# An encoder block in fp32 halves on one core: mixer tiles at a new address, norm 2 and the mixer's operands in a new order, some sums on GpSimd

## The chip, the cores and the metric

The kernel runs on one core of a Trainium2 chip. The metric is the device time of one execution in microseconds (us), as the median of several runs. In the profile PE is TensorE's matmul side, PEld its weight loads, DVE is VectorE, ACT is ScalarE, POOL is GpSimd and SP is SyncE, which issues most of the DMAs.

## What is computed

One layer of a hybrid encoder on 1024 tokens (and 16 meta tokens) of width 1024. The change touches the end of the block alone:

```
h  = h + mix @ w_out              # mix: merged attention and recurrent branches
hn = rmsnorm(h, norm2_g)          # "norm 2"
gu = hn @ w_ffn_in                # 1024 -> 2 x 2816
g, u = gu[..., :D_FF], gu[..., D_FF:]
h  = h + (silu(g) * u) @ w_ffn_out
```

## The kernel before

Every matrix product is made of three matmuls: each fp32 operand is split into a rounded high half (`hi`, by ACT) and a remainder (`lo = source - hi`, by DVE, or by GpSimd where the helper `split` is told so), and the product is hi\*hi + hi\*lo + lo\*hi. All three are matmuls of a 128x128 stationary operand (the weights of PE) with a 128x512 moving operand.

The program runs in stages: projections and the recurrent branch (to about 490 us of the span), attention (490 to 820 us), the output projection `w_out` with norm 2 (797 to 918 us), the mixer's first half `ffn_in` (918 to 1340 us), and its second half (1340 to 1550 us). The names in the trace:

- The output projection adds to the residual rows of token tile t (0 to 7, 128 tokens each) in four parts: two column halves n and two contraction halves kh. Its PSUM tiles are `oph`, `S` and `ops`, and DVE adds each to `h`.
- `norm2_rows(t)` norms the eight tiles one by one (`ss`, `nv`, `ns`, `nr`, `ne` are its small columns, `y` its result). PE then transposes `y` into two PSUM tiles `hT`.
- The mixer uses Strassen's scheme in Winograd's form (7 products in place of 8). The lower tokens (tiles 0 to 3) give the operands B11 and B21 directly (`B`). For each upper tile (4 to 7), `norm2_T` makes c1 to c4 and c22 out of the transposed rows and the lower tile's values, which GpSimd first puts together again from their halves (`whole`), and splits them into T1 to T4 and B22 (`T`, `B`).
- For each of 22 blocks f of 128 mixer columns, `prep(f)` loads the weights (`raw`), forms the sums s1 to s4 (`s`) and splits seven weight operands (`wA`, `wS`). `early(f)` makes the two products that need only the lower tokens (A11 with B11, A12 with B21); `ffn_in(f)` makes the other five (S2 with T2 first, then S3, S1, A22, S4). A product is 12 matmuls.
- The second half of the mixer has the products `po`, whose two operands both lie in one page `pw`.

The normed tokens `xn` lie in two chunks: the first has the 16 meta tokens ahead of its 512 (rows of 528 columns), the second 512 alone. The projections `gm`, `gr` and others of the early stages use both in turn, with one set of weights `wblk`.

The big operands lie in 15 *pages* of SBUF (`xn`, `wblk`, `M`, `wo`, `B`, `T`, `pw`). The mixer's weights lie in a pool of 12 tiles `t4` (4 KB per partition), its temporaries in a pool of 10 tiles `t2`. The order of the instructions on each engine is the one in which the program was built: an engine waits with its next instruction until that can run. Before the change the eight tiles are normed one per output tile in the last eight output tiles, `norm2_T` follows one tile behind, and the two products of `early` for the blocks 0 and 1 stand ahead of the last two `norm2_T`.

Of the kernel before, what the change touches and what calls it, by code (L numbers as in the profile page):

```python
# [8 lines left out]
F32 = mybir.dt.float32  # L9
# [4 lines left out]
ALU = mybir.AluOpType  # L14
# [12 lines left out]
DFF = 2816  # L27
# [8 lines left out]
N_PAGES = 15  # L36
N_T4 = 12
N_T2 = 10


@with_exitstack
def tile_hybrid_encoder_block(
# [258 lines left out]
    ys = [norm1_rows(0)]  # L301
# [219 lines left out]
    for b in range(NB):  # L521
# [5 lines left out]
        w = next_block()  # L527
# [139 lines left out]
    def out_half(t, n, kh, ps):  # L667

        c, o = t // 4, 128 * (t % 4)
        for j in range(2):  # L670
            w = wo[2 * kh + j, n]
            for k in range(2):
                lh, ll = (M[hl][kh][c][:, 2 * j + k, o:o + 128] for hl in range(2))
                PE.matmul(out=ps, lhsT=lh, rhs=w[:, k, 0], start=(j == 0 and k == 0), stop=False)
                PE.matmul(out=ps, lhsT=lh, rhs=w[:, k, 1], start=False, stop=False)
                PE.matmul(out=ps, lhsT=ll, rhs=w[:, k, 0], start=False, stop=(j == 1 and k == 1))
            if j == 1:
                hs = hres[t][:, 512 * n:512 * n + 512]
                V.tensor_tensor(out=hs, in0=hs, in1=ps, op=ALU.add)
            yield  # L680
# [43 lines left out]
    for _ in steps:  # L724
        pass
    load_mix(0, 1)
    for k in range(8):
        if k % 2 == 0 and pend:
            u = pend.pop(0)
            emit_pv(*u, gar[u[0]])  # L730
        for _ in out_half(k % 4, k // 4, 1, SB[k // 3][:, k % 3] if k < 6 else fill_bank("oph")):
            pass
    load_mix(1, 1)

# [16 lines left out]
    def t2(name):  # L751
        return p3.tile([128, 512], F32, tag="t2", bufs=N_T2, name=name)

# [11 lines left out]
    def hb(name):  # L765
        if name not in HB:
            HB[name] = [page([128, 4, 512], F32R, f"{name}{hl}") for hl in range(2)]
        return HB[name]
# [3 lines left out]
    def norm2_rows(t):  # L772
        y = t4([128, D], F32, "y2")
        norm_rows(hres[t], 128, g2b, y)
        SP.dma_start(out=h_d[t], in_=hres[t])
        return y

    def norm2_T(t, y):
        o = slice(128 * (t % 4), 128 * (t % 4) + 128)
        ps = []  # L780
        for kh in range(2):
            p = bank("hT")
            for k in range(4):
                kk = 4 * kh + k
                PE.transpose(out=p[:, 128 * k:128 * k + 128], in_=y[:, 128 * kk:128 * kk + 128], identity=ident)
            ps.append(p.rearrange("p (k t) -> p k t", k=4))
        if t < 4:
            for n, nm in enumerate(("B11", "B21")):
                hi, lo = hb(nm)
                split(ps[n], hi[:, :, o], lo[:, :, o])  # L790
            return
        b12, b22 = ps

        def tmp(name):
            return t2(name).rearrange("p (k t) -> p k t", k=4)

        def whole(nm):
            b = tmp("whole")
            hi, lo = hb(nm)
            G.tensor_tensor(out=b, in0=f32(hi)[:, :, o], in1=f32(lo)[:, :, o], op=ALU.add)  # L800
            return b

        b11, b21 = whole("B11"), whole("B21")

        def put(nm, src):
            hi, lo = hb(nm)
            split(src, hi[:, :, o], lo[:, :, o])

        c22 = tmp("c22")
        S.activation(out=c22, in_=b22, func=AF.Copy)  # L810
        c1 = tmp("c1")
        V.tensor_tensor(out=c1, in0=b12, in1=b11, op=ALU.subtract)
        c2 = tmp("c2")
        V.tensor_tensor(out=c2, in0=c22, in1=c1, op=ALU.subtract)
        c3 = tmp("c3")
        V.tensor_tensor(out=c3, in0=c22, in1=b12, op=ALU.subtract)
        c4 = tmp("c4")
        V.tensor_tensor(out=c4, in0=b21, in1=c2, op=ALU.subtract)
        for nm, src in (("T2", c2), ("T3", c3), ("T1", c1), ("T4", c4), ("B22", c22)):
            put(nm, src)  # L820

    def out_tile(t, n, kh):
        for _ in out_half(t, n, kh, bank("ops")):
            pass

    for t in range(4, 8):
        hres[t] = t4([128, D], F32, "h")
        SP.dma_start(out=hres[t], in_=x[128 * t:128 * t + 128])
    for n in range(2):
        for t in range(4, 8):  # L830
            out_tile(t, n, 0)
    ys = []

    def lagged(lag):
        while len(ys) > lag:
            norm2_T(*ys.pop(0))

# [4 lines left out]
    act_d = [dram.tile([7, 128, 512], F32, name=f"act_d{j}") for j in range(NFP)]  # L842
    wot_d = [dram.tile([4, 128, 512], F32, name=f"wot_d{j}") for j in range(NFP)]

    def wsplit(f, nm, src):
        w = t4([128, 2, 512], F32R, "w" + nm)
        split(src, w[:, 0], w[:, 1])
        W[f, nm] = w

    def prep(f):  # L850

        raw = []
        for col in (128 * f, DFF + 128 * f):
            r = raw_tile([128, 8, 128])
            SP.dma_start(out=r, in_=w_ffn_in[:, col:col + 128].rearrange("(k p) c -> p k c", p=128))
            raw.append(r.rearrange("p k c -> p (k c)"))
        a11, a12 = raw[0][:, 0:512], raw[0][:, 512:1024]
        a21, a22 = raw[1][:, 0:512], raw[1][:, 512:1024]
        wsplit(f, "A11", a11)
        yield  # L860
        wsplit(f, "A12", a12)
        yield
        s1 = t2("s1")
        V.tensor_tensor(out=s1, in0=a21, in1=a22, op=ALU.add)
        s2 = t2("s2")
        V.tensor_tensor(out=s2, in0=s1, in1=a11, op=ALU.subtract)
        wsplit(f, "S2", s2)
        yield
        s3 = t2("s3")
        V.tensor_tensor(out=s3, in0=a11, in1=a21, op=ALU.subtract)  # L870
        wsplit(f, "S3", s3)
        yield
        wsplit(f, "S1", s1)
        yield
# [94 lines left out]
    def step_prep(f, n=1):  # L969
        if f >= NF:  # L970
            return
        if f not in preps:
            preps[f] = prep(f)
        for _ in range(n):
            next(preps[f], None)

    for t in range(8):
        if t < 7:
            ys.append((t, norm2_rows(t)))
        out_tile(4 + t // 2, t % 2, 1)  # L980
        lagged(1)
        if t == 3:
            step_prep(0, 2)
            step_prep(1, 2)
    ys.append((7, norm2_rows(7)))
    for f in range(2):
        for _ in early(f):
            pass
    lagged(0)
    step_prep(0, 5)  # L990

    for f in range(NF):
# [47 lines left out]
    for n, (i, j) in enumerate(chunks):  # L1040
        if n + AHEAD < len(chunks):
            c = chunks[n + AHEAD]
            pairs[c] = load_pair(*seq[c[0]][:2], c[1])
        w = pairs.pop((i, j))
# [94 lines left out]
```

## Time and profile before

| | us |
|---|---|
| median of 3 runs | 1557.53 (1557.37 to 1559.59) |
| profiled execution, its own time | 1556.03 |
| profiled execution, span of the trace | 1554.3 |
| PE, DVE, ACT, POOL busy in the span | 1493.4, 1094.5, 748.4, 305.9 |
| PE busy from 897 to 918 us | 2.93 of 21.00 |

The span is from the first to the last instruction; 1.7 us of the execution lie around it. A busy PE is not PE at its peak: matmuls overlap each other, and what tells how fast they go is the distance between the starts of two that follow each other, which the text calls the pitch.

### The profile page before, as it was taken

The numbers are of one execution on the slowest core, as the hardware profiler recorded it, in microseconds if no ns is written. First come the engines' busy times: TensorE is split into PE (matmuls) and PEld (weight loads), VectorE is DVE, ScalarE is ACT, GpSimd is POOL, SyncE is SP. The second block draws the span as 40 slices with busy tenths as digits, with TensorE's granted clock in tenths as the row PEclk, the third lists the DMA queues.
The fourth block names the chain that finished last, engine by engine and source line by source line (L and its number), as shares of the span: only waits on it lengthen the run. The fifth ranks groups of instructions, "written<-read, shape, count | busy, mean of one in ns | idle before, by whom it ended". The sixth has DMA issues, their size and how long they took to land.

```text
span 1554.3 us, 20204 instructions
## 1 busy us (share of the span) xinstructions
PE 1493.4 (96%) x7323; PEld 1240.6 (80%) x7323; DVE 1094.5 (70%) x1726; ACT 748.4 (48%) x1266; POOL 305.9 (20%) x229
## 2 busy tenths in 40 slices
PE   6999999999999899998989959999999999999998
PEld 4888888888888788887878848888888888888887
DVE  6888677777776778776754788777777777557562
ACT  5544476666666666665632352323332233364330
POOL 0000000000001444444430203333332333300000
PEclk9999999999999999999999979999999999999999
DMA  6123311111112899999995115444444444798541
GB/s 238 42 78 99 89 41 62 61 61 59 60 55 72 181 202 198 201 197 246 229 237 193 41 42 183 161 156 156 152 151 153 154 153 151 256 386 275 192 160 66
DMA packets 307076, 228.92 MB, mean 147 GB/s; under 512 B 150968, under 2 KB 249232, under 8 KB 306976
## 3 DMA queue, kind: packets, MB, share of 16 engines
q1 hardware_dynamic: 303008, 219.77, 49.7%
q0 software_dynamic: 3968, 7.86, 1.8%
q8 instruction: 57, 0.93, 0.3%
q14 instruction: 43, 0.35, 0.1%
HBM read 135.57 MB, written 56.36 MB: 123 GB/s over the span
## 4 chain that ended last, share of the span: by engine, by line
PE 47%; DVE 2%; DMA 1%; issue 0%; ACT 0%; DVEq 0%
PE po L1055 4%; PE po L1053 4%; PE po L1054 4%; PE S2T L889 1%; PE S2T L887 1%; PE S2T L888 1%; PE S3T L889 1%; PE A22T L889 1%; PE S1T L889 1%; PE S4B L889 1%; PE S4B L888 1%; PE A22T L888 1%; PE S1T L888 1%; PE S3T L888 1%; PE S3T L887 1%; PE S4B L887 1%
## 5 line engine op out<-in xcount | busy, mean ns | idle before, releaser
L594 DVE SCALAR_TENSOR_TENSOR PP<-p,pr,PP 128x1024 f16<-128x1024 f32 (+1 forms) x128 | 120.1, 991 | 18.7 <-ACT PP L591 18.6
L93 ACT ACTIVATE pw<-pr 128x1024 fp32r<-128x1024 f32 x77 | 80.6, 1062 | 104.7 <-PE po L1055 72.2
L93 ACT ACTIVATE wS<-s 128x512 fp32r<-128x512 f32 x88 | 53.1, 628 | 161.3 <-DVE s L870 62.1
L1053 PE MATMUL po<-pw 128*128 128x512 f32 x308 | 119.8, 389 | 0.0
L1055 PE MATMUL po<-pw 128*128 128x512 f32 x308 | 119.8, 389 | 0.0
L1054 PE MATMUL po<-pw 128*128 128x512 f32 x308 | 119.8, 389 | 0.0
L608 PE MATMUL pv<-PT,vt 128*128 128x256 f16 x800 | 99.3, 284 | 17.5 <-DMA PT<-PP 17.5
L94 DVE TENSOR_TENSOR pw<-pr,pw 128x1024 fp32r<-128x1024 f32 x77 | 91.8, 1226 | 32.8 <-ACT pw L93 31.0
L608 PEld LDWEIGHTS <-vt 128*128 128x128 f16 x800 | 78.7, 102 | 34.2 <-issue 18.4
L585 ACT ACTIVATE p<-S,nm 128x1044 f32<-128x1044 f32 x64 | 72.2, 1128 | 66.7 <-DVE nm L582 63.9
L94 DVE TENSOR_TENSOR wS<-s,wS 128x512 fp32r<-128x512 f32 x88 | 70.7, 824 | 19.4 <-ACT wS L93 18.3
L591 ACT ACTIVATE PP<-p,pr 128x1040 f16<-128x1040 f32 x64 | 73.9, 1155 | 13.4 <-DMA PT<-PP 8.7
L582 DVE TENSOR_REDUCE nm<-S 128x1 f32<-128x1044 f32 x64 | 76.9, 1231 | 2.4 <-PE S L101 2.3
L430 POOL MEMSET xrp<- 128x2 f32 x8 | 0.9, 109 | 350.2 <-DVE xc L437 350.2
L99 PE MATMUL S<-kT,qh 128*128 128x348 f32 (+1 forms) x192 | 63.1, 328 | 5.6 <-ACT p L585 5.5
L1054 PEld LDWEIGHTS po<-pw 128*128 128x128 f32 x308 | 57.8, 188 | 12.1
L1055 PEld LDWEIGHTS po<-pw 128*128 128x128 f32 x308 | 57.8, 188 | 12.0
L1053 PEld LDWEIGHTS po<-pw 128*128 128x128 f32 x308 | 57.8, 188 | 11.9
L94 DVE TENSOR_TENSOR wA<-raw,wA 128x512 fp32r<-128x512 f32 x66 | 58.5, 886 | 7.3 <-ACT wA L93 7.3
L100 PE MATMUL S<-kT,qh 128*128 128x348 f32 (+1 forms) x192 | 62.2, 324 | 0.0
L101 PE MATMUL S<-kT,qh 128*128 128x348 f32 (+1 forms) x192 | 62.0, 323 | 0.0
L100 PE MATMUL xr<-xn,wblk 128*128 128x264 f32 (+1 forms) x192 | 61.4, 320 | 0.0
(304 smaller groups left out, 4443.3 us busy)
## 6 DMA issues: line engine op xcount, KB each, us to landing
raw<-in_w_in_dram SPq DMA_DIRECT2D x44, 512.0 KB, 3.9
raw<-in_w_ffn_in_dram SPq DMA_DIRECT2D x44, 512.0 KB, 4.7
pr<-act_d SPq DMA_DIRECT2D x77, 256.0 KB, 5.2
raw<-in_w_ffn_out_dram SPq DMA_DIRECT2D x22, 512.0 KB, 4.0
wot_d<-bs SPq DMA_DIRECT2D x44, 256.0 KB, 4.5
act_d<-as SPq DMA_DIRECT2D x44, 256.0 KB, 2.0
pr<-wot_d SPq DMA_DIRECT2D x44, 256.0 KB, 5.1
act_d<-act SPq DMA_DIRECT2D x33, 256.0 KB, 3.5
```

Source lines behind the costliest of these rows:

```text
L93: S.activation(out=hi, in_=src, func=AF.Copy)
L94: (eng or V).tensor_tensor(out=lo, in0=src, in1=f32(hi), op=ALU.subtract)
L100: PE.matmul(out=ps, lhsT=lh, rhs=rl, start=False, stop=False)
L582: V.tensor_reduce(out=nm, in_=s[:, :, 0:KC], axis=AX.XY, op=ALU.max, negate=True)
L591: S.activation(out=pair[:, 0:NK], in_=pf, func=AF.Copy, scale=r)
L594: V.scalar_tensor_tensor(out=pair[:, o:o + e - a], in0=pf[:, a:e], scalar=r, in1=pair[:, a:e], op0=ALU.mult, op1=ALU.subtract)
L608: PE.matmul(out=ps, lhsT=vt[:, j, hl, vs], rhs=pt[:, m], start=(n == 0), stop=(n == len(terms) - 1))
L888: PE.matmul(out=ps, lhsT=lh, rhs=bl[:, k], start=False, stop=False)
L889: PE.matmul(out=ps, lhsT=ll, rhs=bh[:, k], start=False, stop=k == 3)
L1053: PE.matmul(out=banks[t], lhsT=lh, rhs=w[:, 0, 1], start=j == 0, stop=False)
L1054: PE.matmul(out=banks[t], lhsT=lh, rhs=w[:, 1, 1], start=False, stop=False)
L1055: PE.matmul(out=banks[t], lhsT=ll, rhs=w[:, 0, 1], start=False, stop=j == NFP - 1)
```

## The change

Four things are done.

1. A tile of 96 bytes that nobody uses is put into a small pool, ahead of the pools that hold `raw`, the keys and values, and the mixer's `t4` and `t2`. By the addresses in the two built programs, the start of these tiles in a partition, as bytes past a multiple of 256, moves so:

| tiles | before | after |
|---|---|---|
| all pages (`xn`, `wblk`, `M`, `wo`, `B`, `T`, `pw`, `qh`) | 192 | 192 |
| `t4`, `t2` (`wA`, `wS`, `act`, `s`, `c`, `whole`), `raw`, `kT` | 96 | 192 |
| `PP` (probabilities, source of the DMA transposes), `PT` (their result) | 128, 64 | 224, 160 |
| `gw`, `xch` (the recurrent gates' weights and input) | 128, 96 | 224, 192 |

2. Four output tiles move from the attention stage's PSUM banks behind the end of that stage. The lower tiles 0 to 3 are normed first, all four of them, before the last 16 output tiles, and their transposes lie between output tiles. The upper tiles follow one per two output tiles.
3. The weights A11 and A12 of the blocks 0, 1 and 2 (`N_EARLY`) are split ahead of the others, their `lo` on GpSimd in place of DVE, and the two early products of all three blocks, six products, stand between the last transposes, ahead of the first product S2 with T2. For these three blocks A11 and A12 are loaded a second time, for the sums.
4. For each upper tile the sum c4 and the `lo` of T4 move from DVE to GpSimd; c1 and c4 are written over `whole`. T2 and T3 are split first, the rest (`T1`, `T4`, `B22`) after other work.

```diff
@@ small pool
+    small.tile([128, 24], F32, bufs=1, name="shift")
@@ end of the attention stage
-    for k in range(8):
+    for k in range(4):
...
-        for _ in out_half(k % 4, k // 4, 1, SB[k // 3][:, k % 3] if k < 6 else fill_bank("oph")):
+        for _ in out_half(k, 0, 1, SB[k // 3][:, k % 3]):
@@ operands of the upper tiles
-        b11, b21 = whole("B11"), whole("B21")
...
+        c1, c4 = whole("B11"), whole("B21")
         c22 = tmp("c22")
         S.activation(out=c22, in_=b22, func=AF.Copy)
-        c1 = tmp("c1")
-        V.tensor_tensor(out=c1, in0=b12, in1=b11, op=ALU.subtract)
+        V.tensor_tensor(out=c1, in0=b12, in1=c1, op=ALU.subtract)
...
-        c4 = tmp("c4")
-        V.tensor_tensor(out=c4, in0=b21, in1=c2, op=ALU.subtract)
-        for nm, src in (("T2", c2), ("T3", c3), ("T1", c1), ("T4", c4), ("B22", c22)):
-            put(nm, src)
+        G.tensor_tensor(out=c4, in0=c4, in1=c2, op=ALU.subtract)
+        put("T2", t, c2)
+        put("T3", t, c3)
+        yield
+        put("T1", t, c1)
+        put("T4", t, c4, G)
+        put("B22", t, c22)
@@ output tiles, norm 2, early products
-    for n in range(2):
-        for t in range(4, 8):
-            out_tile(t, n, 0)
+    ys = {}
+    for t in range(4):
+        out_tile(t, 1, 1)
+        ys[t] = norm2_rows(t)
+    for t in range(4, 8):
+        out_tile(t, 0, 0)
...
+    def prep_early(f):
+        for nm, a in zip(("A11", "A12"), load_win(128 * f)):
+            wsplit(f, nm, a, G)
...
-    for t in range(8):
-        if t < 7:
-            ys.append((t, norm2_rows(t)))
-        out_tile(4 + t // 2, t % 2, 1)
-        lagged(1)
-        if t == 3:
-            step_prep(0, 2)
-            step_prep(1, 2)
-    ys.append((7, norm2_rows(7)))
-    for f in range(2):
-        for _ in early(f):
-            pass
-    lagged(0)
-    step_prep(0, 5)
+    for t in range(4):
+        out_tile(4 + t, 1, 0)
+        norm2_lower(t, ys.pop(t))
+    upper = {}
+    for t in range(4, 8):
+        for n in range(2):
+            out_tile(t, n, 1)
+        ys[t] = norm2_rows(t)
+        if t < 6:
+            prep_early(t - 4)
+        else:
+            upper[t - 2] = norm2_upper(t - 2, ys.pop(t - 2))
+            next(upper[t - 2])
...
+    run(early(0))
+    prep_early(2)
+    run(upper[4])
+    upper[6] = norm2_upper(6, ys.pop(6))
+    next(upper[6])
+    run(upper[5])
+    run(early(1))
+    step_prep(0, 1)
+    run(upper[6])
+    upper[7] = norm2_upper(7, ys.pop(7))
+    next(upper[7])
+    run(early(2))
+    step_prep(0, 1)
+    run(upper[7])
+    step_prep(0, 5)
```

What stands on DVE for the last upper tile, t = 7, before the change, from its first sum c1 (`c<-hT,whole`) on; the S2 weights of block 0 (`s`, then `wS`) come behind it:

```order
L812 TENSOR_TENSOR c_8373<-hT,whole 128x512
L94 TENSOR_TENSOR B_8164<-c_8371,B_8163 128x4x128
L814 TENSOR_TENSOR c_8375<-c_8371,c_8373 128x512
L816 TENSOR_TENSOR c_8377<-c_8371,hT 128x512
L818 TENSOR_TENSOR c_8379<-whole,c_8375 128x512
L94 TENSOR_TENSOR T_8148<-c_8375,T_8147 128x4x128
L94 TENSOR_TENSOR T_8152<-c_8377,T_8151 128x4x128
L94 TENSOR_TENSOR T_8156<-c_8373,T_8155 128x4x128
L94 TENSOR_TENSOR T_8160<-c_8379,T_8159 128x4x128
L864 TENSOR_TENSOR s_8391<-raw 128x512
L866 TENSOR_TENSOR s_8393<-s_8391,raw 128x512
L870 TENSOR_TENSOR s_8398<-raw 128x512
```

On DVE for the same tile now, from its c1 (written over `whole`) on:

```order
L818 TENSOR_TENSOR whole<-hT,whole 128x512
L820 TENSOR_TENSOR c_8386<-c_8383,whole 128x512
L97 TENSOR_TENSOR wS_8360<-s_8358,wS_8360 128x512
L822 TENSOR_TENSOR c_8388<-c_8383,hT 128x512
L97 TENSOR_TENSOR T_8161<-c_8386,T_8160 128x4x128
L97 TENSOR_TENSOR T_8278<-whole,T_8277 128x4x128
L97 TENSOR_TENSOR T_8165<-c_8388,T_8164 128x4x128
L907 TENSOR_TENSOR act<-p_8408,A12B_8410 128x512
L884 TENSOR_TENSOR s_8426<-raw 128x512
L97 TENSOR_TENSOR B_8286<-c_8383,B_8285 128x4x128
L892 TENSOR_TENSOR s_8443<-raw,s_8358 128x512
L97 TENSOR_TENSOR wS_8428<-s_8426,wS_8428 128x512
```

c4 and the `lo` of T4 have left DVE. The sums s1 and s2 that make S2 stood behind all splits of the tile; now they stand ahead of its c1 (some rows above these), and the `lo` of S2 (`wS`, third row) ahead of the tile's splits.

GpSimd before, from the first `whole` to the first sum of the mixer's other weights (`bs`): nothing but the eight sums.

```order
L800 TENSOR_TENSOR whole<-B_7933,B_7934 128x512
L800 TENSOR_TENSOR whole<-B_7937,B_7938 128x512
L800 TENSOR_TENSOR whole<-B_7933,B_7934 128x512
L800 TENSOR_TENSOR whole<-B_7937,B_7938 128x512
L800 TENSOR_TENSOR whole<-B_7933,B_7934 128x512
L800 TENSOR_TENSOR whole<-B_7937,B_7938 128x512
L800 TENSOR_TENSOR whole<-B_7933,B_7934 128x512
L800 TENSOR_TENSOR whole<-B_7937,B_7938 128x512
L961 TENSOR_TENSOR bs<-raw 128x512
```

GpSimd now, from the first `whole` of tile 6 on; `whole<-whole,c` is c4, `T` the `lo` of T4, `wA` the `lo` of the early weights of block 2:

```order
L812 TENSOR_TENSOR whole<-B_7898,B_7899 128x512
L823 TENSOR_TENSOR whole<-whole,c_8229 128x512
L812 TENSOR_TENSOR whole<-B_7902,B_7903 128x512
L97 TENSOR_TENSOR T_8282<-whole,T_8281 128x4x128
L97 TENSOR_TENSOR wA_8271<-raw,wA_8271 128x512
L97 TENSOR_TENSOR wA_8274<-raw,wA_8274 128x512
L823 TENSOR_TENSOR whole<-whole,c_8306 128x512
L97 TENSOR_TENSOR T_8282<-whole,T_8281 128x4x128
L812 TENSOR_TENSOR whole<-B_7898,B_7899 128x512
L812 TENSOR_TENSOR whole<-B_7902,B_7903 128x512
L823 TENSOR_TENSOR whole<-whole,c_8386 128x512
L97 TENSOR_TENSOR T_8282<-whole,T_8281 128x4x128
```

GpSimd's part of the stage has grown from 8 instructions to 22, and c4 of one tile now stands between the two `whole` of a later tile, so that a late c2 on DVE holds up the next tile's `whole`, for which DVE waits in turn.

## Rows read from the trace of the kernel before

**Rows 1.** The page: span, and busy time of each engine

```profile
span 1554.3 us, 20204 instructions
PE 1493.4 (96%) x7323; PEld 1240.6 (80%) x7323; DVE 1094.5 (70%) x1726; ACT 748.4 (48%) x1266; POOL 305.9 (20%) x229
```

**Rows 2.** Busy time by stretch: length, engines (instructions), granted clock, DMA share, GB/s

```profile
490.00:820.00 330.00, 305.86 (x1874) 264.18 (x1873) 244.97 (x373) 205.60 (x333) 148.88 (x107) 0.96 0.98 204
897.00:918.00 21.00, 2.93 (x16) 2.29 (x15) 17.36 (x31) 14.14 (x22) 1.82 (x2) 0.64 0.06 26
917.70:923.40 5.70, 5.61 (x13) 3.99 (x14) 4.92 (x8) 2.21 (x5) 0.00 (x0) 0.50 0.59 180
985.00:1340.00 355.00, 355.00 (x1523) 285.57 (x1522) 261.73 (x359) 108.13 (x180) 112.11 (x72) 1.00 0.48 161
1341.00:1549.00 208.00, 208.00 (x920) 172.21 (x919) 112.50 (x118) 76.24 (x76) 7.99 (x4) 1.00 0.62 216
```

**Rows 3.** Timeline of PE at the handover: start, length, instruction [idle before <-releaser]

```profile
896.72 1.04 PE L785 MATMUL hT<-ident,y 128*128 128x128 f32 x8
903.68 1.97 PE L785 MATMUL hT<-ident,y 128*128 128x128 f32 x8 [5.93 <-DVE y L135]
917.79 0.79 PE L887 MATMUL S2T<-T,wS 128*128 128x512 f32 x1 [12.14 <-ACT wS L93]
...
923.37 0.45 PE L887 MATMUL S3T<-T,wS 128*128 128x512 f32 x1
...
926.24 0.39 PE L887 MATMUL S1T<-T,wS 128*128 128x512 f32 x1
...
929.04 0.39 PE L887 MATMUL A22T<-T,wA 128*128 128x512 f32 x1
```

**Rows 4.** Timeline of PE: first and last of 24 matmuls, two chunks of one projection

```profile
303.06 0.40 PE L99 MATMUL gm<-xn,wblk 128*128 128x512 f32 x1
...
308.41 0.39 PE L101 MATMUL gm<-xn,wblk 128*128 128x512 f32 x1
308.64 0.40 PE L99 MATMUL gm<-xn,wblk 128*128 128x512 f32 x1
...
313.87 0.39 PE L101 MATMUL gm<-xn,wblk 128*128 128x512 f32 x1
```

**Rows 5.** Timeline of PE in the mixer's second half: two matmuls, twelve apart

```profile
1399.81 0.39 PE L1053 MATMUL po<-pw 128*128 128x512 f32 x1
...
1402.53 0.39 PE L1053 MATMUL po<-pw 128*128 128x512 f32 x1
```

**Rows 6.** Groups by line and form: one of 21 groups of `ffn_in`, busy, mean ns

```profile
L887 PE MATMUL S1T<-T,wS 128*128 128x512 f32 x88 | 34.5, 392 | 0.0
```

**Rows 7.** Groups by line and form on DVE and POOL: busy us, mean ns of one

```profile
L94 DVE TENSOR_TENSOR wS<-s,wS 128x512 fp32r<-128x512 f32 x88 | 70.7, 824 | 19.4 <-ACT wS L93 18.3
L94 DVE TENSOR_TENSOR wA<-raw,wA 128x512 fp32r<-128x512 f32 x66 | 58.5, 886 | 7.3 <-ACT wA L93 7.3
L866 DVE TENSOR_TENSOR s<-s,raw 128x512 f32<-128x512 f32 x22 | 23.9, 1088 | 0.5
L935 DVE TENSOR_TENSOR act<-act,c22f 128x512 f32<-128x512 f32 x22 | 20.7, 940 | 14.0 <-ACT act L934 14.0
L930 DVE TENSOR_TENSOR act<-act,u 128x512 f32<-128x512 f32 x22 | 15.1, 684 | 0.0
L947 POOL TENSOR_TENSOR as<-act 128x512 f32<-128x512 f32 x11 | 19.6, 1780 | 184.3 <-DMA act_d<-act 101.4 <-DVE act L935 82.9
```

**Rows 8.** Timeline of DVE and POOL during norm 2

```profile
878.35 1.28 DVE L135 SCALAR_TENSOR_TENSOR y<-h,nr,g2b 128x1024 f32<-128x1024 f32 x1
879.55 0.68 DVE L679 TENSOR_TENSOR h<-h,ops 128x512 f32<-128x512 f32 x1
...
884.39 0.15 DVE L123 RECIPROCAL nr<-ns 128x1 f32<-128x1 f32 x1
884.47 0.67 DVE L94 TENSOR_TENSOR T<-c,T 128x512 fp32r<-128x512 f32 x1
...
890.12 1.78 DVE L814 TENSOR_TENSOR c<-c,c 128x512 f32<-128x512 f32 x1
...
893.02 2.48 DVE L94 TENSOR_TENSOR T<-c,T 128x512 fp32r<-128x512 f32 x4
...
887.82 3.53 POOL L800 TENSOR_TENSOR whole<-B,B 128x512 f32<-128x512 f32 x2 [15.88 <-DVE nr L127]
```

**Rows 9.** Attention: the transposing DMAs (issue to landing), and the waits for them

```profile
PT<-PP SPq DMA_TRANSPOSE x64, 4.9
PE pv L608 <- DMA PT<-PP: 17.5, 6, 7.2
```

More of the change, by code (lines that the diff above doesn't have):

```diff
@@ L38 @@
 N_T2 = 10
+N_EARLY = 3
 @with_exitstack
@@ L776, in norm2_rows, with hn_T @@
         return y
-    def norm2_T(t, y):
-        o = slice(128 * (t % 4), 128 * (t % 4) + 128)
+    def hn_T(t, y):
         ps = []
@@ L786, in norm2_T, with put, norm2_lower, norm2_upper @@
             ps.append(p.rearrange("p (k t) -> p k t", k=4))
[L787 to L792, printed above, removed]
+        return ps
+    def put(nm, t, src, eng=None):
+        o = slice(128 * (t % 4), 128 * (t % 4) + 128)
+        hi, lo = hb(nm)
+        split(src, hi[:, :, o], lo[:, :, o], eng)
+    def norm2_lower(t, y):
+        for nm, p in zip(("B11", "B21"), hn_T(t, y)):
+            put(nm, t, p)
+    def norm2_upper(t, y):
+        b12, b22 = hn_T(t, y)
+        o = slice(128 * (t % 4), 128 * (t % 4) + 128)
         def tmp(name):
@@ L801, in whole @@
             return b
-        b11, b21 = whole("B11"), whole("B21")
-        def put(nm, src):
-            hi, lo = hb(nm)
-            split(src, hi[:, :, o], lo[:, :, o])
+        c1, c4 = whole("B11"), whole("B21")
         c22 = tmp("c22")
         S.activation(out=c22, in_=b22, func=AF.Copy)
-        c1 = tmp("c1")
-        V.tensor_tensor(out=c1, in0=b12, in1=b11, op=ALU.subtract)
+        V.tensor_tensor(out=c1, in0=b12, in1=c1, op=ALU.subtract)
         c2 = tmp("c2")
@@ L828, in tile_hybrid_encoder_block @@
         SP.dma_start(out=hres[t], in_=x[128 * t:128 * t + 128])
-    for n in range(2):
-        for t in range(4, 8):
-            out_tile(t, n, 0)
[L832 to L836, printed above, removed]
+    ys = {}
[4 more added lines that the diff above has]
+        out_tile(t, 0, 0)
     W = {}
@@ L843, in tile_hybrid_encoder_block, with wsplit, load_win @@
     wot_d = [dram.tile([4, 128, 512], F32, name=f"wot_d{j}") for j in range(NFP)]
-    def wsplit(f, nm, src):
+    def wsplit(f, nm, src, eng=None):
         w = t4([128, 2, 512], F32R, "w" + nm)
-        split(src, w[:, 0], w[:, 1])
+        split(src, w[:, 0], w[:, 1], eng)
         W[f, nm] = w
-    def prep(f):
[L852 to L862, printed above, removed]
+    def load_win(col):
+        r = raw_tile([128, 8, 128])
+        SP.dma_start(out=r, in_=w_ffn_in[:, col:col + 128].rearrange("(k p) c -> p k c", p=128))
+        r = r.rearrange("p k c -> p (k c)")
+        return r[:, 0:512], r[:, 512:1024]
+    def prep_early(f):
+        for nm, a in zip(("A11", "A12"), load_win(128 * f)):
+            wsplit(f, nm, a, G)
+    def prep(f):
+        a11, a12 = load_win(128 * f)
+        a21, a22 = load_win(DFF + 128 * f)
+        if f >= N_EARLY:
+            wsplit(f, "A11", a11)
+            yield
+            wsplit(f, "A12", a12)
+            yield
         s1 = t2("s1")
@@ L975, in step_prep, with run @@
             next(preps[f], None)
-    for t in range(8):
-        if t < 7:
-            ys.append((t, norm2_rows(t)))
-        out_tile(4 + t // 2, t % 2, 1)
-        lagged(1)
-        if t == 3:
-            step_prep(0, 2)
-            step_prep(1, 2)
-    ys.append((7, norm2_rows(7)))
-    for f in range(2):
-        for _ in early(f):
-            pass
-    lagged(0)
+    for t in range(4):
[11 more added lines that the diff above has]
+            next(upper[t - 2])
+    def run(g):
+        for _ in g:
+            pass
+    run(early(0))
[12 more added lines that the diff above has]
+    run(upper[7])
     step_prep(0, 5)
```

## The prediction

> **What bounds the kernel now.** The page first: PE is busy for 1493.4 us of 1554.3; apart from its own weight loads, which overlap, nothing is busy for over 70% [rows 1]. So the time is PE's: how fast its matmuls follow each other, and where it stands still. The table by stretch says where to look. From 985 to 1340 us and from 1341 to 1549 us PE has no idle time at all, at the full granted clock; from 897 to 918 us it works for 2.93 us of 21.00 [rows 2]. The timeline of that hole shows two waits [rows 3]: 5.93 us for `y` of the last token tile, 12.14 us for the first weights of the mixer, S2. [...]
>
> The second place is the pitch. A product of 12 matmuls takes 2.80 us in the mixer's first half, 233.3 ns each; in its second half twelve take 1402.53 - 1399.81 = 2.72 us, 226.7 ns [rows 5]. Same shapes, same types, same clock, no idle time in either. What differs is where the operands lie: in the second half both are in one page; in the first the weights are `t4` tiles at 96 bytes past a multiple of 256, the moving operand a page at 192. The earlier stages hold a test of that. In one projection, with one set of weights, the first chunk of tokens has rows of 528 columns (2112 bytes), so that the moving operand starts at 0, 64, 128 or 192 depending on the row, with the weights at 192; in the second chunk all start at 192. The first takes 308.41 - 303.06 = 5.35 us for 23 pitches, 232.6 ns; the second 313.87 - 308.64 = 5.23 us, 227.4 ns [rows 4]. Nothing else differs between the two. So I read it as: equal offsets of the two operands make the fast pitch.
>
> **Part 1, the addresses.** The change puts `t4` at 192, equal to the pages. The first half has 21 groups of 88 matmuls (7 products, three lines each) [rows 6], 1848 in all. At 227.1 ns, between the two fast pitches above, each saves 6.2 ns: **11.5 us**. Bounds: with 226.7 ns 12.2 us; nothing, if the offset is not the cause; a loss is excluded here by the rows, since 233.3 ns already is the slow one of the two levels seen. The faster PE needs nothing that is short: DVE is busy for 262 us of 355 there, DMA for 0.48 [rows 2]. The other tiles that move: the recurrent gates' operands are unequal before (96 and 128) and after (192 and 224), 0; of the keys' twelve operand starts one is equal to the queries' 192 before, and one after, 0 (bound: 576 matmuls by the 6 ns of above, 3.4 us to either side); `PP` and `PT` have a rival below.
>
> [...]
>
> **Part 2, the handover.** Before, PE has no gap up to the end of the transposes at 896.72 + 1.04 = 897.76 us [rows 3], with four early products made and one set of transposes left. After the change the same output tiles are made, and one set of transposes (0.9 us) and two more products (2 x 2.73) stand ahead of S2: PE would be ready for it at 897.76 + 6.3 = 904.1, less 0.3 for the faster pitch of the early products: 903.8 us. From the end of tile 4's transposes to there lie two output tiles, three sets of transposes and six products, 8 x 2.72 + 3 x 0.87 = 24.4 us; so those end at 879.4.
>
> From then on DVE makes all upper operands. Its order, from c1 of tile 4 to the `lo` of T2 of tile 7 (after which S2 can run), has 46 rows: 32 of 512 elements, 2 `y`, 12 of one column. In a dense run the first follow at 0.60 us (four in 2.48, with 0.08 of overlap), `y` at 879.55 - 878.35 = 1.20, the small ones at 0.08 [rows 8]: 19.2 + 2.4 + 1.0 = 22.6 us. Alone, that is within the 24.2 us that PE leaves.
>
> But GpSimd has 13 instructions in that stretch where it had four (`whole`). While it works, a DVE instruction with two operands in SBUF waits: c2 took 1.78 us where its like take 0.68, in the middle of two `whole` [rows 8]. The groups of the mixer give the mean price: `wS` has 88 x (824 - 684) ns, `wA` 66 x 202, s2 22 x 404, the last product of `act` 22 x 256, against 684 ns for the undisturbed one [rows 7]; 12.3 + 13.3 + 8.9 + 5.6 = 40.1 us, over 88 GpSimd sums (eight groups of 11 like the `as` row), 0.46 us per GpSimd instruction. 13 x 0.46 = 6.0 us. DVE then ends at 879.6 + 22.6 + 6.0 = 908.2, and S2 starts there, 4.4 us after PE is ready. Behind it S3 needs seven more DVE instructions (two splits, the early product's sum, s3, B22, s4, the split of S3: 4.2 us) and loses 0.9 to c4 and T4 on GpSimd: 5.1 us. S2 itself takes 2.7 us at the high clock and 5.6 at the low one, so S3 starts 5.1 to 5.6 us behind it either way, at about 913.5. Before: 923.37, with two products (5.6 us) fewer made. **Gain 9.9 + 5.6 = 15.5 us.**
>
> Bounds: if GpSimd's work falls into gaps, S2 starts at 903.8 and S3 at 908.0: 21.0 us. If each of the 13 costs what c2 lost, 1.1 us, S2 starts at 916.5, S3 at 922.1 with the low clock: 6.9 us. I take the mean price, since it is the mean over the same kinds of instructions.
>
> At no cost: the sums and splits that leave DVE for the first three blocks (PE is not waiting for DVE from 985 us on); three loads of 512 KB made twice, on a DMA share of 0.48 [rows 2]; the lower tiles' norms, done while PE has 16 output tiles (44 us) ahead of it. If that cover fails, a wait of the kind of `y`, 5.93 us [rows 3].
>
> **Sum.** 1556.0 (the profiled execution's own time, span 1554.3 and 1.7 around it) - 11.5 - 15.5 = 1529.0 us. It stands 1.5 us under the median of the runs, so 1530.5 us as a median.
>
> **Rivals.**
> - *The offset does nothing* (something else sets the pitch in the first half, such as its denser DVE and ACT traffic). For it: the first half has more DVE work than the second. Against: rows 4, where traffic is the same. 1557.5 - 15.5 = 1542.
> - *The lock between GpSimd and DVE eats the handover.* GpSimd's 13 are a chain of their own: c4 of a tile waits for DVE's c2, and the next `whole` stands behind it. With the upper price the gain is 6.9: 1557.5 - 11.5 - 6.9 = 1539.
> - *Better than the sum*: GpSimd falls into DVE's gaps, 21.0 and 12.2: 1524.
> - *Slower: the transposing DMAs of attention.* There DMA is busy for 0.98 of the 330 us, and PE already waits for them for 17.5 us [rows 2, 9]. 64 of them read `PP`, now at 224 in place of 128, and land after 4.9 us. If the new offset lengthens each by d and PE sees it each time, 64 d is lost; from d = 27.0 / 64 = 0.42 us on it eats the gain, and at d = 0.6 us the time is 1557.5 - 27.0 + 38.4 = 1569. Against it: PE waited in six places only, and PE is busy for 306 of the 330 us, so that most of a small d is covered. [...]
>
> **How the numbers follow.** Both parts as summed, within some 5 us: 0.60. The lock eats the handover: 0.18. The offset does nothing: 0.08 (with the lock's upper price as well, 1551, still faster). Better: 0.08. Transposes: 0.06, half of it slower, half within 0.2%. The likeliest is **1530.5 us**. The range reaches down to the better case and up past the two rivals that lose a part: 1523 to 1545, which leaves out about 0.15. About 0.2% (3 us) is what a measurement of this kernel can tell from no change: faster 0.94, same 0.03, slower 0.03.
>
> **What would show it.** Part 1: a product of the first half takes 2.72 us from S3 of block 0 on, and the 21 groups' means fall to about 389 ns, as `po` has. Part 2: S2 starts within a few us of the end of six early products, with one wait of some 4 us ahead of it and none for `y`; two-operand DVE instructions of 1.2 to 1.8 us between the upper tiles' splits. Wrong would be: products still at 2.80 us; S2 later than 915; waits of `pv` for `PT` in attention well over 17.5 us.

## The result and the profile after

The changed kernel takes 1540.68 us (median of 4 runs, 1539.1 to 1543.0) against 1557.45 us in the same session: a ratio of 0.9892, 95% interval 0.9875 to 0.991. The range held it; the point forecast, 1530.5 us, was 10 us too low. The profiled execution took 1543.0 us, the longest of the four; its span is 13.05 us shorter than before.

The page, span and busy time of each engine:

```profile
span 1541.2 us, 20211 instructions
PE 1484.2 (96%) x7323; PEld 1241.6 (81%) x7323; DVE 1101.1 (71%) x1712; ACT 743.1 (48%) x1264; POOL 325.3 (21%) x243
```

The table by stretch (columns as in [rows 2]): the handover, the stretch behind its last wait, the mixer's first half, and the start of its second half:

```profile
897.00:918.00 21.00, 12.45 (x45) 9.60 (x44) 20.90 (x26) 11.45 (x20) 13.97 (x10) 0.80 0.09 26
917.00:922.00 5.00, 4.95 (x12) 3.89 (x13) 5.00 (x7) 2.21 (x5) 1.53 (x1) 0.50 0.00 0
985.00:1320.00 335.00, 335.00 (x1479) 277.40 (x1478) 257.00 (x349) 100.41 (x174) 112.22 (x72) 1.00 0.48 157
1325.00:1335.00 10.00, 8.93 (x32) 7.07 (x33) 8.39 (x10) 6.36 (x7) 0.00 (x0) 0.83 1.04 369
```

From 897 to 918 us PE now works for 12.45 us where it worked for 2.93, and DVE is busy for 20.90 of 21.00 us (17.36 before), ACT for 11.45: DVE is what is short here. Behind the wait the granted clock is 0.50, as it was behind the wait before [rows 2]. From 985 us on PE has no gap, as before. The last row is new: at the start of the second half PE stands still for 1.07 us of these ten and the granted clock falls to 0.83 in the mean.

The timeline of PE: the handover, two first matmuls of successive products in the middle of the first half, and the start of the second half:

```profile
892.48 1.07 PE L787 MATMUL hT<-ident,y 128*128 128x128 f32 x8 [1.75 <-DVE y L138]
...
904.49 1.97 PE L787 MATMUL hT<-ident,y 128*128 128x128 f32 x8 [5.45 <-DVE y L138]
...
915.66 0.50 PE L901 MATMUL S2T<-T,wS 128*128 128x512 f32 x1 [2.21 <-ACT T L96]
917.05 0.79 PE L902 MATMUL S2T<-T,wS 128*128 128x512 f32 x1 [0.89 <-DVE T L97]
...
921.91 0.63 PE L901 MATMUL S3T<-T,wS 128*128 128x512 f32 x1
...
1201.23 0.39 PE L901 MATMUL S1T<-T,wS 128*128 128x512 f32 x1
...
1203.95 0.39 PE L901 MATMUL A22T<-T,wA 128*128 128x512 f32 x1
...
1325.31 0.49 PE L1086 MATMUL po<-pw 128*128 128x512 f32 x1 [1.51 <-ACT pw L96]
1326.57 0.80 PE L1087 MATMUL po<-pw 128*128 128x512 f32 x1 [0.77 <-DVE pw L97]
```

Against [rows 3]: 10.3 us of waits in place of 18.07, and S3 at 921.91 in place of 923.37, with six early products behind it instead of four. A product takes 1203.95 - 1201.23 = 2.72 us, as `po` does [rows 5]. `po` waits for its first `pw`, which it did not before. S2's first matmul is released by ACT, but ACT began that `hi` of T2 0.3 us after DVE had made c2 (914.70 us).

**Where the 13.05 us come from.** S3 starts 1.46 us earlier. From S3 to the end of the first half (1340.79 us before, 1323.79 after) 417.4 us became 401.9: two products fewer (5.6), 147 products at 2.722 in place of 2.80 us (11.5), less 1.6 for the low clock (0.50) and short gaps just behind S3. From there to the end of the span 213.5 us became 217.4: 3.9 lost. 1.46 + 5.6 + 11.5 - 1.6 - 3.9 = 13.1.

The timeline of POOL and of DVE in the handover:

```profile
876.33 2.54 POOL L97 TENSOR_TENSOR wA<-raw,wA 128x512 fp32r<-128x512 f32 x2 [4.10 <-ACT wA L96]
878.82 1.30 POOL L812 TENSOR_TENSOR whole<-B,B 128x512 f32<-128x512 f32 x1
...
889.52 1.73 POOL L812 TENSOR_TENSOR whole<-B,B 128x512 f32<-128x512 f32 x1 [0.63 <-DVE nr L130]
...
897.84 1.73 POOL L97 TENSOR_TENSOR T<-whole,T 128x512 fp32r<-128x512 f32 x1
899.52 3.01 POOL L97 TENSOR_TENSOR wA<-raw,wA 128x512 fp32r<-128x512 f32 x2
...
914.85 1.60 POOL L823 TENSOR_TENSOR whole<-whole,c 128x512 f32<-128x512 f32 x1 [2.69 <-DVE c L820]
...
876.58 1.07 DVE L127 TENSOR_TENSOR ne<-nr 128x1 f32<-128x1 f32 x1
...
878.16 0.72 DVE L128 TENSOR_TENSOR ne<-ne,nv 128x1 f32<-128x1 f32 x1
...
879.11 1.03 DVE L130 TENSOR_TENSOR nr<-nr,ne 128x1 f32<-128x1 f32 x1
...
881.97 0.69 DVE L818 TENSOR_TENSOR whole<-hT,whole 128x512 f32<-128x512 f32 x1
...
890.04 2.30 DVE L138 SCALAR_TENSOR_TENSOR y<-h,nr,g2b 128x1024 f32<-128x1024 f32 x1
...
898.35 1.23 DVE L127 TENSOR_TENSOR ne<-nr 128x1 f32<-128x1 f32 x1
...
900.10 1.21 DVE L128 TENSOR_TENSOR ne<-ne,nv 128x1 f32<-128x1 f32 x1
...
903.16 1.27 DVE L138 SCALAR_TENSOR_TENSOR y<-h,nr,g2b 128x1024 f32<-128x1024 f32 x1
...
915.82 1.18 DVE L97 TENSOR_TENSOR T<-c,T 128x512 fp32r<-128x512 f32 x1
```

Read the lengths against [rows 8]: a `y` of 1.28 us took 2.30 beside a `whole` that began at 889.52; even rows of one column with two operands, 0.15 us each, took 1.2. From c1 of tile 4 (881.97) to the `lo` of T2 of tile 7 (it ends at 917.0) the 46 rows together are 11.1 us over their undisturbed lengths (0.68 us for 512 elements, 1.28 for `y`, 0.15 for one column), beside 14 instructions of GpSimd, and DVE is idle for 1.05 us. The expectations below count 10.8 us, 0.77 us for each of the 14.

### The profile page after: what moved, and what is told of

Read it like the earlier page. It is cut to its first block, busy times and chain, and to the rows that moved or that the text cites. A ratio compares the mean times of both kernels' runs of the same rounds, so it can differ in the third digit from the quotient of the medians.

```text
span 1541.2 us, 20211 instructions
## 1 busy us (share of the span) xinstructions
PE 1484.2 (96%) x7323; PEld 1241.6 (81%) x7323; DVE 1101.1 (71%) x1712; ACT 743.1 (48%) x1264; POOL 325.3 (21%) x243
## 5 line engine op out<-in xcount | busy, mean ns | idle before, releaser
L611 PE MATMUL pv<-PT,vt 128*128 128x256 f16 x800 | 97.7, 281 | 17.6 <-DMA PT<-PP 16.9
L611 PEld LDWEIGHTS <-vt 128*128 128x128 f16 x800 | 78.0, 101 | 33.5 <-issue 18.3
L97 DVE TENSOR_TENSOR wS<-s,wS 128x512 fp32r<-128x512 f32 x88 | 70.5, 818 | 16.9 <-ACT wS L96 16.0
L594 ACT ACTIVATE PP<-p,pr 128x1040 f16<-128x1040 f32 x64 | 73.9, 1155 | 15.2 <-DMA PT<-PP 10.3
L97 DVE TENSOR_TENSOR wA<-raw,wA 128x512 fp32r<-128x512 f32 x60 | 50.3, 842 | 15.9 <-ACT wA L96 15.9
```

Of the source, the lines that this page charges most:

```text
L594: S.activation(out=pair[:, 0:NK], in_=pf, func=AF.Copy, scale=r)
L611: PE.matmul(out=ps, lhsT=vt[:, j, hl, vs], rhs=pt[:, m], start=(n == 0), stop=(n == len(terms) - 1))
```

## The experiments

The theory that the experiments test: the address part is right; the handover is late since DVE, which alone makes the operands, loses some 0.8 us to every instruction of GpSimd beside it; and a third thing, the wait of `po`, costs some 4 us. Its rivals: another modulus of the offset, the order of the rows, PE's own waits.

### Addresses alone, order alone

The kernel before with the tile:

```diff
+    small.tile([128, 24], F32, bufs=1, name="shift")
```

> The kernel before with the tile of 96 bytes alone; the order of the work stays as it was. If equal offsets of a matmul's two operands make the fast pitch, all 154 products of the mixer's first half take 2.72 us in place of 2.80 from the first block on (226.7 in place of 233.3 ns per matmul) and PE is 12.2 us shorter. A second theory adds to it: the weights' preparation goes round three raw buffers in about 38.4 us per pair of blocks, and PE's new period is 38.1 us, so that the preparation stops running a whole block ahead and the second half starts with a wait of 2 to 4 us for its first pw. With it 1547 to 1550 us, without it 1545.3 us. If the offset does nothing: 1557.5 us and products of 2.80 us.

Measured: 1545.29 us (1544.38 to 1550.31), ratio 0.9928 (0.9911 to 0.9945): 12.4 us less. Two first matmuls of successive products in its timeline:

```profile
1201.44 0.39 PE L889 MATMUL A12B<-B,wA 128*128 128x512 f32 x1
...
1204.16 0.39 PE L889 MATMUL S2T<-T,wS 128*128 128x512 f32 x1
```

2.72 us. The second theory missed: `po` did not wait here. The preparation (end of its last sum s4 to the start of S4) ran 12.4 us ahead at block 0 and 17.1 at block 21.

The changed kernel without the tile:

```diff
-    small.tile([128, 24], F32, bufs=1, name="shift")
```

> The kernel after without the tile of 96 bytes: the new order alone, all addresses as before. If the handover gains what its trace in the changed kernel shows (S3 starts 1.5 us earlier and two products of 2.8 us more stand ahead of it, less some 1.5 us of low clock and short gaps behind S3), 1551 to 1553 us, with products of 2.80 us, and, since PE's period of 39.2 us per pair is longer than the 38.4 us of the raw buffers, no wait at the start of the second half. By the sum on record (15.5 us for the handover) it would be 1542 us. If the order had gained nothing and the addresses all: 1557.5 us.

Measured: 1551.66 us (1547.75 to 1553.91), ratio 0.9961 (0.9947 to 0.9974): 6.1 us less than before, not 15.5. Products take 2.80 us, `po` has no wait. The two parts sum to 18.5 us; together they gave 16.8.

### Which modulus

The changed kernel with a larger tile:

```diff
-    small.tile([128, 24], F32, bufs=1, name="shift")
+    small.tile([128, 56], F32, bufs=1, name="shift")
```

> The kernel after with a tile of 224 bytes in place of 96: the mixer's weights then start 64 bytes past a multiple of 256 and the pages 192, so that the two are equal modulo 128 and not modulo 256. If the offset within 128 bytes decides, the products stay at 2.72 us and the time at that of the kernel after, 1540.7 us. If the offset within 256 bytes decides, the products go back to 2.80 us and the time to that of the kernel without the tile, 1551 to 1553 us.

Measured: 1548.39 us (1547.46 to 1550.88), ratio 0.9949 (0.9934 to 0.9964). In its timeline:

```profile
1201.60 0.40 PE L901 MATMUL S2T<-T,wS 128*128 128x512 f32 x1
...
1204.40 0.40 PE L901 MATMUL S3T<-T,wS 128*128 128x512 f32 x1
```

2.80 us: offsets that are equal modulo 128 (64 and 192) are not enough; the fast pitch came where both are 192 modulo 256. The time lies 2.6 us under the expected band, but its interval overlaps that of the kernel without the tile.

### The wait of po

The changed kernel with the rows of `w_ffn_out` in a page:

```diff
-            w = raw_tile([128, D])
+            w = wopage[:, f % 2]
             SP.dma_start(out=w, in_=w_ffn_out[128 * f:128 * f + 128])
...
+    wopage = page([128, 2, D], F32, "wopg")
     for f in range(NF):
```

> The kernel after with the w_ffn_out rows of a pair of blocks loaded into the one page that is free in the mixer's first half, in place of two of the three raw buffers' turns. If the loop over the raw buffers holds the preparation back, its lead over PE stays at 15 to 20 us up to the last block (8.3 us in the kernel after), the first two po have no wait for pw (1.51 and 0.77 us before, some 4.2 us with the low clock behind them), and the time falls to 1536.5 to 1538.5 us. If the wait comes from the loads of the second half themselves (their order on the queue, their landing), the time stays at 1540.7 us and the wait remains.

Measured: 1536.98 us (1536.78 to 1537.36), ratio 0.987 (0.9855 to 0.9886): 3.7 us less than the changed kernel (the two intervals touch). From the end of the first half to the end of the span it is 213.2 us in place of 217.4. The timeline of SP's queue in the changed kernel, up to the first load `pr` of the second half:

```profile
1312.09 0.33 SPq L972 DMA_DIRECT2D raw<-in_w_ffn_out_dram  x1
...
1317.89 2.81 SPq L955 DMA_DIRECT2D wot_d<-bs  x3
1320.82 0.36 SPq L1043 DMA_DIRECT2D pr<-act_d  x1
```

SP's wait ahead of the first of these rows (its total from 1280 to 1330 us, times, longest):

```profile
SPq L972 <- DVE wA L97: 5.4, 1, 5.4
```

The timeline of the queue in this kernel:

```profile
1294.38 5.70 SPq L955 DMA_DIRECT2D wot_d<-bs  x4
1303.06 0.32 SPq L955 DMA_DIRECT2D act_d<-act  x1
1303.48 0.38 SPq L1044 DMA_DIRECT2D pr<-act_d  x1
```

In the changed kernel the rows of `w_ffn_out` wait on SP for a raw buffer, which DVE frees with its split of A22 at 1312.05; their sums, the stores of the sums and only then the loads of the second half stand behind. With a place of its own the first `pr` is issued 17 us earlier, the preparation leads by 18.3 us at the last block (8.3 in the changed kernel, 19.3 before), and no `po` waits. So the third thing is the raw buffers. Neither part alone loses the lead. With the new order it starts at 9.0 us (12.4 with the addresses alone, 13.6 before); with the order alone, at the slow pitch, it climbs from 8.1 to 19.3, but in the changed kernel it never passes 12.9. Why it then falls there and climbs to 17.1 with the addresses alone, at the same pitch, these runs do not settle.

From here on the kernel with the page is the base. Executions of one kernel spread by up to 7.5 us, and part of that arises in attention (its last `pv` ends between 818.5 and 824.4 us in these profiles), so the handover is read from each profile as a stage: from the end of the last output tile to S2's second matmul, the first that needs the `lo` of T2. "Excess" is what DVE's rows in it take over the undisturbed lengths given above; "GpSimd instructions" are those that reach into the stage.

| kernel | median us | stage us | GpSimd instructions | excess us |
|---|---|---|---|---|
| changed | 1540.68 | 32.65 | 14 | 11.1 |
| + page | 1536.98 | 32.65 | 14 | 11.1 |
| + c4, T4 on DVE | 1535.60 | 32.25 | 6 | 5.0 |
| + early `lo` on DVE | 1531.89 | 26.75 | 4 | 2.7 |
| the last with nine idle sums | 1541.39 | 35.65 | 13 | 10.7 |
| page, no `whole` | 1536.09 | 29.39 | 10 | 7.8 |
| page, early products first | 1541.31 | 35.36 | 15 | 12.4 |

### GpSimd's sums back on DVE

The kernel with the page, and:

```diff
-        G.tensor_tensor(out=c4, in0=c4, in1=c2, op=ALU.subtract)
+        V.tensor_tensor(out=c4, in0=c4, in1=c2, op=ALU.subtract)
...
-        put("T4", t, c4, G)
+        put("T4", t, c4)
```

> The kernel with the w_ffn_out page (1537.0 us), and the sum c4 and the lo of T4 of all four upper tiles back on DVE: eight instructions fewer on GpSimd, eight more on DVE. In the trace of the changed kernel, DVE's rows from c1 of tile 4 to the lo of T2 of tile 7 lose 10.8 us beside 14 instructions of GpSimd, 0.77 us each. If that price holds, DVE saves 8 x 0.77 = 6.2 us and does 8 x 0.60 = 4.8 us more: S3 starts 1.4 us earlier and the time is 1535.5 us. By the mean price of the prediction, 0.46 us, DVE would save 3.7 and do 4.8 us more: 1538 us. If GpSimd costs DVE nothing: 1541.8 us.

Measured: 1535.6 us (1535.22 to 1539.97), ratio 0.9861 (0.9845 to 0.9878), the time expected, though the interval overlaps that of the kernel with the page. In the profile S3 starts 36.3 us after the last output tile in place of 37.5, and the stage is 0.4 us shorter. The excess fell by 6.1 us with eight instructions of GpSimd, 0.76 us each, while nine more rows of 512 elements stand on DVE in the stage.

The same, and:

```diff
-            wsplit(f, nm, a, G)
+            wsplit(f, nm, a)
```

> The same, and the lo of A11 and A12 of the first three blocks on DVE as well: GpSimd keeps only the sums called whole. At 0.77 us each the two of block 2 save 0.3 us more, and the four of blocks 0 and 1, which stand ahead of whole of tile 4, let c1 of tile 4 start up to 2.4 us earlier (881.97 us in the changed kernel, 879.6 in the prediction): 1533 to 1535.5 us. By the mean price of 0.46 us: 1539 us.

Measured: 1531.89 us (1529.32 to 1534.48), ratio 0.9831 (0.9813 to 0.985), 8.8 us under the changed kernel and 1.1 us under the band expected. The timeline of DVE and of PE at the handover:

```profile
881.50 0.15 DVE L127 TENSOR_TENSOR ne<-nr 128x1 f32<-128x1 f32 x1
...
884.19 1.27 DVE L138 SCALAR_TENSOR_TENSOR y<-h,nr,g2b 128x1024 f32<-128x1024 f32 x1
...
908.49 0.80 PE L901 MATMUL S2T<-T,wS 128*128 128x512 f32 x1 [6.62 <-ACT T L96]
909.63 0.79 PE L902 MATMUL S2T<-T,wS 128*128 128x512 f32 x1 [0.35 <-DVE T L97]
```

No transposes wait for `y` any more: the last ones end at 896.42 us, and what is left is one wait for T2. The stage is 5.5 us shorter than in the run above: the excess fell by 2.3 us and four rows of 512 elements fewer (2.4 us) fall into it, since c1 of tile 4 now starts 4.7 us ahead of the end of the last output tile (1.4 us in the run above).

### The price by itself

The last kernel with sums on GpSimd that nobody reads, one each behind T2, T3 and T1 of three tiles:

```diff
+    def idle_sum(nm, t):
...
+        G.tensor_tensor(out=nobody, in0=f32(hi)[:, :, o], in1=f32(lo)[:, :, o], op=ALU.add)
...
         put("T2", t, c2)
+        if t < 7:
+            idle_sum("T2", t)
...
```

> The kernel with GpSimd's sums on DVE (1531.9 us), with nine sums on GpSimd added that nobody uses (T2, T3 and T1 of tiles 4 to 6, high plus low half, into the free page). DVE's rows are the same as before, so only GpSimd's working beside DVE can make it later. At the 0.77 us per instruction read from the changed kernel, S2 starts 6.9 us later: 1538.8 us; at the 0.46 us of the prediction 4.1 us: 1536 us; if GpSimd beside DVE costs nothing, 1531.9 us. Up to 1 us may come on top from the whole of tile 7, which stands behind one of the nine.

Measured: 1541.39 us (1538.64 to 1546.12), ratio 0.9901 (0.9882 to 0.9919): 9.5 us more (at most 7.9 were expected), the stage 8.9 us longer, 8.0 of it excess. The timeline of GpSimd and DVE:

```profile
906.93 4.92 POOL L807 TENSOR_TENSOR wopg<-T,T 128x512 f32<-128x512 f32 x3 [5.50 <-DVE T L97]
...
908.98 1.74 DVE L97 TENSOR_TENSOR B<-c,B 128x512 fp32r<-128x512 f32 x1
910.65 0.68 DVE L921 TENSOR_TENSOR act<-p,A12B 128x512 f32<-128x512 f32 x1
911.25 1.15 DVE L892 TENSOR_TENSOR s<-raw 128x512 f32<-128x512 f32 x1
```

Nine sums with no reader cost 1.0 us each. While GpSimd worked, the DVE rows above with two operands in SBUF took 1.74 and 1.15 us, and the one with an operand in PSUM (`A12B`) 0.68. That GpSimd is free beside a DVE without gaps, or costs 0.46 us there, is out.

### Is it the order, or PE's own waits?

The kernel with the page, with the lower tiles' high halves in place of `whole`:

```diff
-        c1, c4 = whole("B11"), whole("B21")
+        b11, b21 = f32(hb("B11")[0])[:, :, o], f32(hb("B21")[0])[:, :, o]
+        c1, c4 = tmp("c1"), tmp("c4")
...
```

What this kernel leaves out: c1 and c4, and with them T1, T2 and T4, lack the low halves of the lower tiles.

> The kernel with the w_ffn_out page (1537.0 us), with the eight sums called whole left out (the upper operands are made from the high halves of the lower ones alone): eight instructions fewer on GpSimd and none more on DVE. If GpSimd slows DVE by 0.77 us per instruction and DVE is what S2 waits for, S3 starts some 5 to 6 us earlier, at 915.5 to 916.5 us of the span, the two-operand rows of DVE in the stretch fall towards 0.68 us, and the time is 1531 to 1532 us; at 0.46 us per instruction 1533.3 us. If the handover is late for another reason (the order of DVE's rows, y behind the small columns), the time stays within 1 us of 1537.

Measured: 1536.09 us (1532.57 to 1536.4), ratio 0.9853 (0.9837 to 0.9869). The median lies within 1 us of 1537 and alone would speak for the rival; in this profile attention ended 2.3 us later than in the base's, and the stage is 3.3 us shorter. The expectation counted eight `whole`, of which only five fall into the stage, 0.65 us each. The size was missed. That GpSimd's sums cost time rests here on the stage of one profile.

The kernel with the page, in another order on PE:

```diff
-    upper[7] = norm2_upper(7, ys.pop(7))
-    next(upper[7])
     run(early(2))
+    upper[7] = norm2_upper(7, ys.pop(7))
+    next(upper[7])
```

> The kernel with the w_ffn_out page (1537.0 us), with the two early products of block 2 put ahead of the transposes of tile 7 in place of behind them. PE then works through its wait of 5.45 us for y of tile 7 and waits ahead of S2 instead. If DVE is the bound from 882 to 917 us and PE's waits there cost nothing of their own, S2 and S3 start where they did within 1 us, and the time is 1536 to 1538 us. If the wait for y is what costs, S3 starts up to 5.4 us earlier: 1532 us.

Measured: 1541.31 us (1539.15 to 1545.84), ratio 0.9901 (0.9883 to 0.9918): later by 4.3 us, by 2.7 us in the stage. The timeline of PE:

```profile
901.59 0.50 PE L903 MATMUL A11B<-B,wA 128*128 128x512 f32 x1 [1.87 <-POOL wA L97]
...
918.23 0.79 PE L901 MATMUL S2T<-T,wS 128*128 128x512 f32 x1 [8.84 <-ACT T L96]
```

Filling PE's wait gained nothing: the time came back ahead of S2, so no sign that the wait for `y` costs by itself. That it got worse was not expected. The transposes of tile 7 now stand behind two more products (908.4 in place of 904.5 us), but no row of DVE waits for them: DVE has two rows of 512 elements more ahead of the `lo` of T2 (33 in place of 31 in the stage, 1.2 us) and 1.3 us more excess. So this run moved DVE's order as well as PE's.

### Towards a better kernel

With the sums on DVE, first the split of B22 of all four tiles behind the operands of S2 (c22 held in the free page):

```diff
+        yield
         put("B22", t, c22)
...
-    run(upper[7])
+    for t in range(4, 8):
+        run(upper[t])
```

> The kernel with GpSimd's sums on DVE (1531.9 us), with c22 of the upper tiles kept in the free page and the split of B22 for all four tiles moved behind the first product S2's operands. Four rows of DVE of 0.60 us leave the stretch ahead of the lo of T2 of tile 7. If DVE is what S2 waits for, S2 starts 2.4 us earlier: 1529.5 us. If something else holds S2 back (PE's order, ACT, a load), 1531 to 1532.5 us.

Measured: 1532.57 us (1527.83 to 1534.03), ratio 0.9833 (0.9814 to 0.9853). The time lies beside the second case, that something else holds S2 back, and the medians do not tell it from 1531.89. The stage speaks for DVE: 24.33 us in place of 26.75, 2.4 us as expected. Then a fourth block's early products in the wait that is left:

```diff
-N_EARLY = 3
+N_EARLY = 4
...
     run(early(1))
+    prep_early(3)
...
     run(early(2))
+    run(early(3))
```

> The kernel with B22 split late, with the two early products of a fourth block ahead of S2. DVE gets three rows more ahead of S2 (two lo and one sum, 1.8 us), PE does 5.4 us of products in a stretch in which it would wait. If PE's wait ahead of S2 is as long as DVE's rows make it, 3.6 us less than without the fourth block: 1526 us, and a little less if S2 then starts at the high clock. If the fourth pair of weights comes too late for PE (buffers, loads), the time stays at that of the kernel without it or above.

Measured: 1526.97 us (1524.83 to 1527.43), ratio 0.9799 (0.9781 to 0.9818). The timeline of PE at S2:

```profile
911.62 0.50 PE L905 MATMUL S2T<-T,wS 128*128 128x512 f32 x1 [0.19 <-ACT T L96]
912.76 0.50 PE L906 MATMUL S2T<-T,wS 128*128 128x512 f32 x1 [0.64 <-DVE T L97]
```

The table by stretch, from S2's second matmul to S3:

```profile
912.70:916.00 3.30, 3.01 (x12) 2.17 (x13) 3.30 (x7) 2.53 (x5) 0.00 (x0) 1.00 0.00 0
```

The stage has two products more and is 1.8 us longer; S2 runs at the full granted clock (1.00), and PE stood still for only 0.19 and 0.64 us ahead of it. This is the best version: 13.7 us under the changed kernel.

## Why the prediction was right and wrong, step by step

- **Part 1, addresses, 11.5 us:** right. From shortly behind S3 of block 0 on, the first half's products take 2.72 us, and alone the tile gave 12.4 us. The reading of [rows 4], one stage's two chunks as a test for another, carried over. Where the two operands lie matters here: 2.72 against 2.80 us per product, with the tile of 96 bytes and without one.
- **Part 2, handover, 15.5 us:** mis-sized; 7.1 us by S3's start and the two products, 6.1 us in the run of the order alone. Three terms. (1) The price of GpSimd: 13 x 0.46 = 6.0 us was 11.1. The 0.46 was a mean over the mixer, where DVE is idle for a quarter of the time [rows 2, 7]. There, from 990 to 1300 us before the change, 64 GpSimd instructions lengthened only 39 DVE rows by more than 0.2 us, 0.77 us each; in the handover, where DVE has hardly a gap, 14 lengthened 13 rows, 0.86 us each. By the runs a GpSimd instruction costs 0.65 to 1.0 us there. The bound of 1.1 us from [rows 8], a row in a dense stretch, was the nearer row. (2) The start: c1 of tile 4 came at 881.97, not 879.6. The two `lo` of A11 and A12 and the first `whole` (876.33 to 880.12) lengthened three one-column rows ahead of it by 2.4 us; I had priced GpSimd's instructions from c1 on only. (3) 1.05 us of idle time on DVE. So 908.2 became 917.0: 5.1 + 2.4 + 1.05, the rest rounding. The count of 46 rows and their 22.6 us were right. The 5.6 us of S2 at the low clock are its 923.37 - 917.79 = 5.58 us before the change [rows 3], at a granted 0.50 [rows 2]; now S3 came 4.9 us behind S2's second matmul, again at 0.50.
- **"None for y":** wrong. Two sets of transposes waited, 1.75 and 5.45 us, because DVE, which makes `y` between its other rows, was late by then; the rows of one column that `y` needs, priced at 0.08 us, got longer beside GpSimd like the long ones (1.23 and 1.21 us at 898.35 and 900.10). Filling the longer wait in the run with the early products first gained nothing.
- **"At no cost":** wrong in the loads. The 0.48 share of DMA was no measure of it: the three raw buffers and the order of SP's queue bound the preparation, and its lead, which had hidden them, was 19.3 us at the last block before and 8.3 after. It cost 3.9 us in the profile, and giving the loads a place of their own took 3.7 us away.
- **Rivals:** "the offset does nothing" fell with the first run. "The lock eats the handover" is what happened, in so far as DVE's rows were 11.1 us longer beside GpSimd (the runs show these lengths, not a lock as their cause): S3 at 921.9 us (922.1 there), 1540.7 us (1539 there); it had 0.18 and should have had most. That its S3 fits to 0.2 us is partly chance: its 14.3 us were 13 instructions at 1.1, and what came was 11.1 of price, 2.4 of late start and 1.05 of idle time. Its chain on GpSimd (c4, then the next `whole`) is not needed: the nine sums slow DVE without any reader, by 1.0 us each. The range held the result because it reached past this rival, not because the sum was right. "Slower transposes": they land after a median of 5.1 us as against 4.9, and the waits of `pv` are no longer than before in this pair of profiles, as the group by line shows:

```profile
L611 PE MATMUL pv<-PT,vt 128*128 128x256 f16 x800 | 97.7, 281 | 17.6 <-DMA PT<-PP 16.9
```

16.9 us after, 17.5 before [rows 9]. Over all profiles the waits of `pv` together vary from 16.0 to 20.6 us with the tile of 96 bytes, and are 14.6 and 17.5 without a tile, so that a loss of a microsecond or two is not excluded. The packets did not get longer with `PP` 224 bytes past a multiple of 256 in place of 128: from 500 to 800 us those of 256 bytes took 18 ns in the median before and after, 24.6 and 24.4 in the mean.

## What to carry to other kernels

Price a slowed engine by a row from a stretch as dense as the one in question; a mean over a stage with gaps hid nearly half of it here. Moving a two-operand sum from a full DVE to GpSimd gains nothing here: it saves 0.60 us and costs 0.65 to 1.0. When the bounding engine gets faster, look at the lead of what feeds it, buffer by buffer, not at busy shares.

## What the hardware showed unexpectedly

- In the mixer's first half TensorE's pitch at 128x512 fp32r went with where weights and moving operand start in a partition: 226.7 ns where both start 192 bytes past a multiple of 256 (the changed kernel, and the kernel before with the tile), 233.3 ns where the weights start 96 (before) or 64 bytes past one (the larger tile; 64 and 192 are equal modulo 128). Whether other equal offsets are as fast, no run shows.
- Beside GpSimd even DVE's two-operand rows of 128x1 took up to 1.25 us (886.42, changed kernel) in place of 0.15.
- With two more early products in the wait the granted clock did not fall: from its second matmul to S3, S2 took 921.91 - 917.05 = 4.9 us in the changed kernel, at 0.50, behind waits of 2.21 and 0.89 us; with the fourth block's products ahead of it 915.82 - 912.76 = 3.1 us, at 1.00, behind waits of 0.19 and 0.64 us.
